# Retention units whose next scores are made before the last group-norm scaling

## The chip, the cores and the metric

One Trainium2 chip, one of its cores, float32 throughout. The metric is device time in microseconds (us) of one execution. TensorE is PE in the rows (PEld its weight loads), VectorE DVE, ScalarE ACT, GpSimd POOL; SP and ACT issue the DMAs. All engines run their own instruction streams in order and wait for one another by semaphores.

## The reference

A trunk of two layers with a gated MLP after each. The change lies in the second mixer, multi-scale retention: 4 heads, 1024 positions, query and key dimension 256, value dimension 512, a group norm over each head's 512 values, a gate and an output projection.

```python
def retention_mixer(xn, wq, wk, wv, wg, gn_gain, wo):
    q, k, v = ...                        # 4 heads; q and k rotated, k scaled
    o = chunkwise_retention(rotary(q, pos), rotary(k, pos), v)   # decayed causal scores @ v
    mu = jnp.mean(o, axis=-1, keepdims=True)
    var = jnp.mean(jnp.square(o - mu), axis=-1, keepdims=True)
    o = (o - mu) * lax.rsqrt(var + EPS) * gn_gain.astype(jnp.float32)
    o = o.reshape(Bn, S, RET_HEADS * RET_VDIM).astype(xn.dtype)
    return (jax.nn.silu(xn @ wg) * o) @ wo
```

## The kernel before

Each float32 operand of a product is held as a high and a low half (`split`: ScalarE converts the high half, at line 109; GpSimd or VectorE subtracts it to get the low half, at line 110), and each product is three passes: high x high, high x low, low x high, in this order (`PASSES`; the first name is the half of the stationary operand).

When projections q, k, v and gate are done, retention runs as eight units: for each head h, half 0 (positions 0 to 511) and half 1. One unit, in the order of the program text:

1. `scores` (L1186): four groups of 6 matmuls, 512, 384, 256 and 128 columns wide, each into a PSUM bank of the ring `b` (four banks). VectorE multiplies each by a mask into a tile `s` (L1191; three buffers), and `split` turns it into `sT`.
2. In half 0 only, `key_rows` (L1201: eight transposes into `b` banks, ScalarE and VectorE split them into `ky`) and `first_state` (L1212: 24 matmuls; L1218 and L1219 split the result into `st`), which half 1 uses.
3. `outputs` (L1236): four outputs t = 0 to 3, each in a `b` bank. Output t takes 3(t+1) matmuls, in half 1 six more with `st`. VectorE takes the group-norm statistics (L1240, L1241), GpSimd the inverse root (L152, L153), and VectorE scales the bank into `y` (L1227), one output late: the scaling of t = 3 is the returned function `finish`.
4. `gated`: four groups of four transposes of `y` (L1260) into `b` banks; VectorE multiplies each by gain and gate (L1261); `split` makes `yT`, four blocks c = 0 to 3: the high halves on ScalarE, the low halves of c = 0 and 2 on GpSimd, of 1 and 3 on VectorE.
5. `wo_sweep`: the output projection of this unit as eight steps of 12 matmuls (L328), four steps for blocks 0 and 1 (g = 0), four for blocks 2 and 3. `yT` is the stationary operand; VectorE adds each result into the residual (L333). These steps are not run there: they are the filler of the next unit. `fill(n)` runs n of them, and the tables say where: `SFILL[half]` after scores, after key_rows and after outputs, `OFILL[half]` after each output. `run(steps)` runs those left, just ahead of `gated`.

```python
SFILL = ((1, 1, 2), (1, 0, 2))
OFILL = ((0, 1, 1, 0), (1, 1, 1, 0))
```

The weights of a unit's sweep are eight blocks (`w_rows`, through `load` into `raw`, five buffers, and `hilo` into `hl`, seven buffers). With seven buffers for eight blocks per unit, the fourth block of a unit takes the buffer that the previous unit's fifth leaves, that is, after that unit's last step. A build step places instructions within each engine near the text's order but not exactly in it; the rows of the order below are what stands in the built programs.

Of the kernel before, what the change touches and what calls it, by code (L numbers as in the profile page):

```python
# [41 lines left out]
SFILL = ((1, 1, 2), (1, 0, 2))  # L42
# [32 lines left out]
def trunk(tc, a):  # L75
# [28 lines left out]
    def f(ap):  # L104
        return ap.bitcast(F32)

    def split(hi, lo, src, eng=None):

        act.copy(hi, src)  # L109
        (eng or pool).tensor_tensor(lo, src, f(hi), ALU.subtract)  # L110
# [18 lines left out]
    def hilo(src, into=None, eng=None):  # L129
        hl = wp.tile([P, 2, 512], "hl", HL, F32R) if into is None else into  # L130
        split(hl[:, 0, :], hl[:, 1, :], src, eng)
        return hl
# [5 lines left out]
    def row_block(w, r, c0):  # L138

        return load(w[r * P : (r + 1) * P, c0 : c0 + 512])  # L140
# [5 lines left out]
    def w_rows(w, r):  # L146
        return [hilo(row_block(w, r, hf * 512)) for hf in range(2)]
# [173 lines left out]
    def sweep(lhs, ws, tiles, bank, after=None):  # L321
        n = len(ws)
        for t in tiles:
            for hf in range(2):
                o = bank()
                for j in range(n):
                    for i, (ls, w) in enumerate(PASSES):
                        pe.matmul(  # L328
                            o, lhs[j](ls, t), ws[j][hf][:, w, :],
                            start=(j == 0 and i == 0), stop=(j == n - 1 and i == 2),  # L330
                        )
                xs = xb[:, t, hf * 512 : (hf + 1) * 512]
                dve.tensor_tensor(xs, xs, o, ALU.add)  # L333
            if after:
                after(t)
            yield

    def run(gen):
        for _ in gen:
            pass  # L340
# [294 lines left out]
    def filler():  # L635
        for c in range(4):
            while at["heads"] <= c:
                yield
            yield from gated_conv(c)
        while at["values"] < 4 or at["pairs"] < 3:  # L640
            yield
        vp.close()
        xtp.close()
        mix["mp"] = Pool("mp")
        mix["ab"] = Pool("ab")
        gather((1, 3, 5, 7, 0, 2, 4), mix["ab"])
        for js in ((1, 3), (5, 7)):
            for _ in project(js, (1, 3, 5, 7, 0, 2, 4, 6), u_bank):
                yield from (None,) * 4

    steps = filler()

    def fill(n):
        for _ in range(n):
            next(steps, None)
# [36 lines left out]
    def b_bank():  # L692
        return ps.tile([P, 512], "b", 4)
# [467 lines left out]
    wo = a["ret_wo"][0]  # L1161

    def fetch_q(h, half):
        q = rt[0].tile([P, 2, 2, HALF], "q", 2, dt=F32R)
        sync.dma_start(out=f(q), in_=qscr[4 * h + 2 * half])
        return q

    def fetch_k(h, half):

        k, kf = rt[1].tile([P, 2, 2, HALF], "k", dt=F32R), None  # L1170
        sync.dma_start(out=f(k), in_=qscr[4 * h + 2 * half + 1])
        if half == 0:
            kf = rt[1].tile([P, 2, HALF], "kf")
            sync.dma_start(out=kf, in_=kscr[h])
        return k, kf
# [3 lines left out]
    def scores(q, k):  # L1179
        sT = rt[3].tile([P, 2, 1280], "sT", dt=F32R)  # L1180
        for j in range(4):
            n = HALF - j * P
            b = b_bank()
            for d in range(2):
                for i, (ks, qs) in enumerate(PASSES):
                    pe.matmul(  # L1186
                        b[:, :n], k[:, ks, d, j * P : (j + 1) * P], q[:, qs, d, j * P :],
                        start=(d == 0 and i == 0), stop=(d == 1 and i == 2),
                    )
            t = wk.tile([P, HALF], "s", 3)  # L1190
            dve.tensor_tensor(t[:, :n], b[:, :n], unit0["tri"][:, :n], ALU.mult)  # L1191
            split(sT[:, 0, SOFF[j] : SOFF[j] + n], sT[:, 1, SOFF[j] : SOFF[j] + n], t[:, :n], (pool, dve)[j % 2])
        return sT

    def key_rows(kf):

        kn = rt[3].tile([P, 4, HALF], "ky", dt=F32R).rearrange("p t (s d) -> p t s d", s=2)
        for t in range(4):
            pt = b_bank()
            for d in range(2):  # L1200
                pe.transpose(pt[:, d * P : (d + 1) * P], kf[:, d, t * P : (t + 1) * P], ident)  # L1201
            act.copy(kn[:, t, 0, :], pt[:, :256])
            dve.tensor_tensor(kn[:, t, 1, :], pt[:, :256], f(kn[:, t, 0, :]), ALU.subtract)
        return kn

    def first_state(kn, v):

        pd = [o_bank(), o_bank()]
        for t in range(4):
            for d in range(2):  # L1210
                for i, (ks, vs) in enumerate(PASSES):
                    pe.matmul(  # L1212
                        pd[d], kn[:, t, ks, d * P : (d + 1) * P], v[:, vs, t, :],
                        start=(t == 0 and i == 0), stop=(t == 3 and i == 2),
                    )
        st = rt[3].tile([P, 2, 2, HALF], "st", dt=F32R)
        for d in range(2):
            act.copy(st[:, 0, d, :], pd[d])  # L1218
            dve.tensor_tensor(st[:, 1, d, :], pd[d], f(st[:, 0, d, :]), ALU.subtract)  # L1219
        return st  # L1220
# [28 lines left out]
    def gated(h, y, gt, last):  # L1249
        if last:  # L1250
            t = h_tile()
            yT = [t[:, :, i * HALF : (i + 1) * HALF] for i in range(2)]
            yT += [u_tile().bitcast(F32R).rearrange("p (s t) -> p s t", s=2) for _ in range(2)]
        else:
            t = [yp.tile([P, 2, 2, HALF], f"y{i}", dt=F32R) for i in range(2)]
            yT = [t[c // 2][:, :, c % 2] for c in range(4)]
        for c in range(4):
            pt = b_bank()
            for t in range(4):
                pe.transpose(pt[:, t * P : (t + 1) * P], y[:, t, c * P : (c + 1) * P], ident)  # L1260
            dve.scalar_tensor_tensor(gt[:, c, :], pt, gncol(h, c), gt[:, c, :], ALU.mult, ALU.mult)  # L1261
            split(yT[c][:, 0], yT[c][:, 1], gt[:, c, :], (pool, dve)[c % 2])
        return yT

    def wo_sweep(half, h, yT, g, tiles, after=None):
        def lhs(j):
            return lambda s, t: yT[2 * g + j][:, s, (t - 4 * half) * P : (t - 4 * half + 1) * P]

        return sweep(
            [lhs(j) for j in range(2)], [w_rows(wo, h * 4 + 2 * g + j) for j in range(2)], tiles, o_bank, after  # L1270
        )

    def fetch_v(h, half, queue=act):
        v = rt[4 if half else 2].tile([P, 2, 4, HALF], "v", dt=F32R)
        for s in range(2):
            queue.dma_start(out=f(v[:, s]), in_=vscr[2 * h + half, :, s])
        return v

    def fetch_g(h, half):
        t, ts = rt[3].tile([P, 4, HALF], "gt"), slice(half * HALF, (half + 1) * HALF)  # L1280
        sync.dma_start(out=t, in_=scr[4 * h : 4 * h + 4, :, ts].rearrange("a p t -> p a t"))
        return t
# [25 lines left out]
    for h in range(4):  # L1308
        for n, block in enumerate(blocks):
# [6 lines left out]
            steps = strassen(a[name][0], c0, c0 + P, xc, Both, ((o_bank if n in (1, 4) else b_bank),), us, lay=1)  # L1316
            if h == n == 0:
                steps, us = nxt["head"]
# [10 lines left out]
    q, (k, kf) = unit0["q"], unit0["k"]  # L1329
    v, gt = unit0["v"], fetch_g(0, 0)  # L1330
    steps = iter(())
    for n, (h, half) in enumerate(units):
        more = n + 1 < len(units)
        sT = scores(q, k)
        fill(SFILL[half][0])
        if half == 0:
            kn = key_rows(kf)
            fill(SFILL[half][1])
            st = first_state(kn, v)
        if more:  # L1340
            q2, (k, kf) = fetch_q(*units[n + 1]), fetch_k(*units[n + 1])
        y, finish = outputs(half, q, v, sT, st)
        if more:
            q = q2
            fill(SFILL[half][2])
            v = fetch_v(*units[n + 1])
        finish()
        if more:
            run(steps)
        else:  # L1350
            fill(2)
        yT = gated(h, y, gt, not more)
        if not more:
            run(steps)
            nrm = Norming(a["ffn_norm"][1:2])
            nrm.play("q0 r0 q1")
        if more:
            gt = fetch_g(*units[n + 1])
            tiles = range(4 * half, 4 * half + 4)
            steps = chain(*[wo_sweep(half, h, yT, g, tiles) for g in range(2)])  # L1360
    for p in (yp, rt[4], rt[3], rt[2], rt[1], rt[0]):
        p.close()
    open_xc()
# [54 lines left out]
```

## Time and profile before

| | us |
|---|---|
| median of 3 runs (2721.56 to 2728.98) | 2725.92 |
| the profiled execution | 2726.38 |
| its span, first to last instruction | 2724.6 |
| TensorE busy | 2645.2 (97% of the span) |
| VectorE, ScalarE, GpSimd busy | 1915.8, 1189.9, 795.9 |
| mean granted TensorE clock | 0.993 |

The page gives, engine by engine, the busy time and its share of the span. The timeline lists an engine's instructions in order of time, runs of like ones merged, with the idle time ahead of them and what ended it. Retention's units run from 1708.9 us to about 2027 us. A granted clock of 1.00 is 2.4 GHz, 0.50 is 1.2 GHz.

### The profile page before, as it was taken

The page shows a single profiled execution, that of the slowest core. Times are in us where ns is not written, and L with a number is a line of the kernel's source. Part 1 is how long each engine was busy: PE and PEld are TensorE (multiplying, and loading weights), DVE is VectorE, ACT ScalarE, POOL GpSimd, SP SyncE. Part 2 cuts the span into 40 slices and gives each one's busy share as a digit, 9 for nine tenths or more (in the row PEclk, how much of TensorE's full clock was granted, in tenths as well). Part 3 has the DMA queues.
Part 4 walks back from the last instruction along what each step waited for, and adds up shares of the span by engine and source line. Part 5 has one row for each costly group of instructions (what it writes and reads, how often), then busy time and mean ns, then how long its engine had stood idle before and what let it go on. Part 6 is the DMA issues. An engine that isn't in the chain of part 4 may idle for free. (4 is left out here: it accounts for less than half of the span.)

```text
span 2724.6 us, 34990 instructions
## 1 busy us (share of the span) xinstructions
PE 2645.2 (97%) x12793; PEld 2166.0 (80%) x12793; DVE 1915.8 (70%) x2950; ACT 1189.9 (44%) x2050; POOL 795.9 (29%) x603
## 2 busy tenths in 40 slices
PE   8999999899999999989999999899999999999999
PEld 6877777778888888868888888788877888887887
DVE  4247776687777789697575765466678777777986
ACT  4345543454444444364444434222235444445444
POOL 6721113533333400032222122344454333331000
PEclk9999999999999999999999999899999999999999
DMA  5310012122222274424554546655422222225654
GB/s 171 104 48 28 24 35 79 38 75 89 74 89 74 86 266 154 152 84 160 176 178 151 195 150 219 244 210 186 155 73 60 78 85 72 88 74 187 206 174 154
DMA packets 258785, 336.74 MB, mean 124 GB/s; under 512 B 15121, under 2 KB 182197, under 8 KB 252469
## 3 DMA queue, kind: packets, MB, share of 16 engines
q1 hardware_dynamic: 224428, 246.94, 28.4%
q10 hardware_dynamic: 34184, 87.57, 8.8%
q8 instruction: 100, 1.64, 0.2%
q14 instruction: 73, 0.59, 0.1%
HBM read 257.38 MB, written 77.07 MB: 123 GB/s over the span
## 5 line engine op out<-in xcount | busy, mean ns | idle before, releaser
L110 POOL TENSOR_TENSOR hl<-raw,hl 128x512 fp32r<-128x512 f32 x347 | 580.9, 1688 | 1250.9 <-ACT hl L109 1231.0
L245 PE MATMUL b<-xc,hl 128*128 128x512 f32 (+1 forms) x2652 | 606.2, 388 | 10.7 <-ACT u L305 5.7
L245 PE MATMUL o<-xc,hl 128*128 128x512 f32 (+1 forms) x2568 | 590.7, 389 | 12.9 <-DVE hl L110 3.3
L245 PEld LDWEIGHTS b<-xc,hl 128*128 128x128 f32 x2652 | 485.9, 189 | 125.2 <-ACT u L305 7.0
L245 PEld LDWEIGHTS o<-xc,hl 128*128 128x128 f32 x2568 | 473.4, 190 | 123.6 <-DVE hl L110 4.2
L109 ACT CAST hl<-raw 128x512 fp32r<-128x512 f32 (+1 forms) x440 | 264.9, 609 | 508.7 <-PE o L328 151.7
L110 DVE TENSOR_TENSOR hl<-s,hl 128x512 fp32r<-128x512 f32 x309 | 223.6, 727 | 222.0 <-ACT hl L109 222.0
L972 DVE SCALAR_TENSOR_TENSOR u<-u,cc,u 128x1022 f32<-128x1022 f32 (+1 forms) x176 | 263.4, 1521 | 0.9
L109 ACT CAST hl<-s 128x512 fp32r<-128x512 f32 x309 | 189.7, 619 | 136.8 <-PE b L245 47.2
L458 PE MATMUL u<-xT,hl 128*128 128x512 f32 x576 | 166.1, 410 | 0.0
L328 PE MATMUL o<-hl,y 128*128 128x512 f32 x672 | 163.6, 397 | 0.0
L905 PE MATMUL o<-hl,hl 128*128 128x512 f32 x600 | 146.3, 394 | 5.0 <-DVE hl L110 3.5
L328 PEld LDWEIGHTS o<-hl,y 128*128 128x128 f32 x672 | 125.6, 188 | 29.4 <-POOL y L110 0.2
L905 PEld LDWEIGHTS o<-hl,hl 128*128 128x128 f32 x600 | 111.3, 188 | 34.4 <-DVE hl L110 7.1
L333 DVE TENSOR_TENSOR xb<-xb,o 128x512 f32<-128x512 f32 x160 | 105.0, 680 | 38.0 <-PE o L328 37.9
L458 PEld LDWEIGHTS u<-xT,hl 128*128 128x128 f32 x576 | 99.4, 189 | 20.7 <-issue 5.7
L970 ACT ACTIVATE u<-u,cc 128x1024 f32<-128x1024 f32 x88 | 100.9, 1151 | 31.3 <-DVE u L312 31.3
L109 ACT CAST hl<-h 128x512 fp32r<-128x512 f32 (+1 forms) x124 | 70.0, 581 | 95.0 <-PE o L905 28.2
L1063 PE MATMUL o<-hl,xc 128*128 128x256 f32 x768 | 95.4, 282 | 0.9 <-DVE hl L110 0.8
L1063 PEld LDWEIGHTS o<-hl,xc 128*128 128x128 f32 x768 | 93.8, 188 | 1.8 <-DVE hl L110 1.0
L110 DVE TENSOR_TENSOR hl<-h,hl 128x512 fp32r<-128x512 f32 (+1 forms) x124 | 78.4, 647 | 21.9 <-ACT hl L109 21.7
L152 POOL TENSOR_SCALAR rr<-ss 128x1 f32<-128x1 f32 (+1 forms) x48 | 13.8, 287 | 254.8 <-ACT s L163 235.9
(220 smaller groups left out, 4009.4 us busy)
## 6 DMA issues: line engine op xcount, KB each, us to landing
raw<-in_ffn_w_up SPq DMA_DIRECT2D x176, 256.0 KB, 3.1
raw<-in_ffn_w_down SPq DMA_DIRECT2D x176, 256.0 KB, 3.3
hs<-u ACTq DMA_DIRECT2D x44, 512.0 KB, 2.7
h<-hs SPq DMA_DIRECT2D x44, 512.0 KB, 6.4
raw<-in_even_w_in SPq DMA_DIRECT2D x73, 256.0 KB, 2.8
qscr<-h ACTq DMA_DIRECT2D x16, 1024.0 KB, 4.0
vscr<-u ACTq DMA_DIRECT2D x32, 512.0 KB, 3.8
raw<-in_ret_wo SPq DMA_DIRECT2D x64, 256.0 KB, 3.2
```

The lines of the kernel that those rows point to most:

```text
L109: act.copy(hi, src)
L110: (eng or pool).tensor_tensor(lo, src, f(hi), ALU.subtract)
L152: pool.tensor_scalar(out, ss, 1.0 / n, EPS, ALU.mult, ALU.add)
L245: pe.matmul(u, hl[:, ws, k * P : (k + 1) * P], xc[b][:, xs, k, cols_], start=(first and k == 0 and i == 0), stop=(k == 3 and i == 2), skip ...
L328: pe.matmul(o, lhs[j](ls, t), ws[j][hf][:, w, :], start=(j == 0 and i == 0), stop=(j == n - 1 and i == 2),)
L333: dve.tensor_tensor(xs, xs, o, ALU.add)
L458: pe.matmul(u, hl(ws, k), xT[:, xs, k, hf * 512 : (hf + 1) * 512], start=(k == 0 and i == 0), stop=(k == KT - 1 and i == 2),)
L905: pe.matmul(o, l[:, ls, c * P : (c + 1) * P], r[:, ws, :], start=(start and i == 0), stop=(stop and i == 2), skip_group_check=True,)
L970: act.mul(c, u, wcol(2, jj))
L972: dve.scalar_tensor_tensor(c[:, d:], u[:, :-d], wcol(2 - d, jj), c[:, d:], ALU.mult, ALU.add)
L1063: pe.matmul(u[t // 2][:, c : c + 256], xc[b][:, xs, k, ts], hl[name][k // 2][:, ws, k % 2 * 256 : k % 2 * 256 + 256], start=(first and k = ...
```

## The change

The scores of unit n+1 are made in unit n, behind its four outputs and the two filler steps that follow, and ahead of `finish`. The step that stood behind the scores (`SFILL[half][0]`, one in both halves) now stands behind `finish`. The first scores, and the load and split of the first sweep's four weight blocks, stand ahead of the loop. All else, the tables too, is as it was.

```diff
-    def wo_sweep(half, h, yT, g, tiles, after=None):
+    def wo_sweep(half, h, yT, g, tiles, after=None, ws=None):
         ...
-        return sweep(
-            [lhs(j) for j in range(2)], [w_rows(wo, h * 4 + 2 * g + j) for j in range(2)], tiles, o_bank, after
-        )
+        ws = ws or [w_rows(wo, h * 4 + 2 * g + j) for j in range(2)]
+        return sweep([lhs(j) for j in range(2)], ws, tiles, o_bank, after)
...
     steps = iter(())
+    sT = scores(q, k)
+    ws = [w_rows(wo, j) for j in range(2)]
     for n, (h, half) in enumerate(units):
         more = n + 1 < len(units)
-        sT = scores(q, k)
-        fill(SFILL[half][0])
         if half == 0:
             kn = key_rows(kf)
             fill(SFILL[half][1])
...
             fill(SFILL[half][2])
             v = fetch_v(*units[n + 1])
+            sT = scores(q, k)
         finish()
+        fill(SFILL[half][0])
         if more:
             run(steps)
...
-            steps = chain(*[wo_sweep(half, h, yT, g, tiles) for g in range(2)])
+            steps = chain(*[wo_sweep(half, h, yT, g, tiles, ws=None if n or g else ws) for g in range(2)])
```

TensorE from the last output of unit 0 into unit 1, where no filler step exists yet, before and then after (`b_` names are banks; L1236 outputs, L1260 transposes of `y`, L1186 scores, L328 the sweep):

```order
L1236 MATMUL b_15275<-v_15047,sT_15129 128x512 x12
L1260 MATMUL b_15302<-ident_67,ky_15230 128x128 x3
L1260 MATMUL b_15310<-ident_67,ky_15230 128x128 x3
L1260 MATMUL b_15318<-ident_67,ky_15230 128x128 x3
L1260 MATMUL b_15302<-ident_67,ky_15230 128x128
L1260 MATMUL b_15310<-ident_67,ky_15230 128x128
L1260 MATMUL b_15318<-ident_67,ky_15230 128x128
L1260 MATMUL b_15326<-ident_67,ky_15230 128x128 x4
L1186 MATMUL b_15377<-q_15226,k_15228 128x512 x6
```

```order
L1236 MATMUL b_15295<-v_15047,sT_15129 128x512 x12
L1186 MATMUL b_15320<-q_15246,k_15248 128x512 x6
L1186 MATMUL b_15331<-q_15246,k_15248 128x384 x6
L1186 MATMUL b_15342<-q_15246,k_15248 128x256 x6
L1186 MATMUL b_15353<-q_15246,k_15248 128x128 x6
L1260 MATMUL b_15367<-ident_67,ky_15250 128x128 x4
L1260 MATMUL b_15375<-ident_67,ky_15250 128x128 x4
L1260 MATMUL b_15383<-ident_67,ky_15250 128x128 x4
L1260 MATMUL b_15391<-ident_67,ky_15250 128x128 x4
L1236 MATMUL b_15428<-v_15316,sT_15319 128x512 x3
L1236 MATMUL b_15428<-st_15241,q_15246 128x512 x6
```

The scores moved from behind the transposes of `y` to ahead of them; behind the transposes stand the nine matmuls of unit 1's first output, and the sweep's first step follows them.

TensorE from unit 1's transposes into unit 2 (a first half, so key_rows follow), before and then after:

```order
L1260 MATMUL b_15675<-ident_67,ky_15443 128x128 x4
L1186 MATMUL b_15726<-q_15437,k_15439 128x512 x6
L1186 MATMUL b_15737<-q_15437,k_15439 128x384 x6
L1186 MATMUL b_15748<-q_15437,k_15439 128x256 x6
L1186 MATMUL b_15759<-q_15437,k_15439 128x128 x6
L328 MATMUL o_15770<-hl_15687,y_2777_15649 128x512 x3
L328 MATMUL o_15770<-hl_15697,y_2777_15649 128x512 x3
```

```order
L1260 MATMUL b_15720<-ident_67,ky_15427 128x128 x4
L1201 MATMUL b_15771<-ident_67,kf_15425 128x128 x2
L328 MATMUL o_15791<-hl_15732,y_2786_15694 128x512
L1201 MATMUL b_15776<-ident_67,kf_15425 128x128 x2
L328 MATMUL o_15791<-hl_15732,y_2786_15694 128x512 x2
L1201 MATMUL b_15781<-ident_67,kf_15425 128x128 x2
L328 MATMUL o_15791<-hl_15742,y_2786_15694 128x512 x2
L1201 MATMUL b_15786<-ident_67,kf_15425 128x128 x2
L328 MATMUL o_15799<-hl_15737,y_2786_15694 128x512 x2
```

Between the transposes and the sweep's first step stood 24 matmuls of the scores; now the eight transposes of key_rows stand there, mixed with the step's own matmuls.

GpSimd at the same place, before and then after (`hl` the weights' low halves, `y` the low halves of blocks 0 and 2, `sT` those of the scores):

```order
L110 TENSOR_TENSOR hl_15702<-raw_15700,hl_15702 128x512
L110 TENSOR_TENSOR hl_15707<-raw_15705,hl_15707 128x512
L110 TENSOR_TENSOR hl_15712<-raw_15710,hl_15712 128x512
L110 TENSOR_TENSOR hl_15717<-raw_15715,hl_15717 128x512
L110 TENSOR_TENSOR y_2777_15649<-gt_15334,y_2777_15649 128x512
L110 TENSOR_TENSOR y_2778_15650<-gt_15334,y_2778_15650 128x512
L110 TENSOR_TENSOR sT_15725<-s_15733,sT_15725 128x512
L110 TENSOR_TENSOR sT_15725<-s_15755,sT_15725 128x256
```

```order
L110 TENSOR_TENSOR hl_15747<-raw_15745,hl_15747 128x512
L110 TENSOR_TENSOR hl_15752<-raw_15750,hl_15752 128x512
L110 TENSOR_TENSOR hl_15757<-raw_15755,hl_15757 128x512
L110 TENSOR_TENSOR hl_15762<-raw_15760,hl_15762 128x512
L110 TENSOR_TENSOR y_2786_15694<-gt_15399,y_2786_15694 128x512
L110 TENSOR_TENSOR y_2787_15695<-gt_15399,y_2787_15695 128x512
```

The four weight halves stand ahead of the two `y` halves in both; the `sT` halves moved from behind them to some places ahead (not shown).

ScalarE ahead of unit 0's state, before and then after:

```order
L1202 CAST ky_15174<-b_15190 128x256
L109 CAST hl_15363<-raw_15361 128x512
L109 CAST hl_15368<-raw_15366 128x512
L1218 CAST st_15221<-o_15195 128x512
L1218 CAST st_15221<-o_15196 128x512
```

```order
L1202 CAST ky_15194<-b_15210 128x256
L109 CAST hl_15408<-raw_15406 128x512
L109 CAST hl_15413<-raw_15411 128x512
L1218 CAST st_15241<-o_15215 128x512
L1218 CAST st_15241<-o_15216 128x512
```

Only the names differ: the sixth and seventh weight blocks are converted ahead of the state in both, and SP's queue issues its loads up to there in the same order too.

## Rows read from the trace of the kernel before

**Rows 1.** The page, part 1: busy time, share of span, instructions.

```profile
PE 2645.2 (97%) x12793; PEld 2166.0 (80%) x12793; DVE 1915.8 (70%) x2950; ACT 1189.9 (44%) x2050; POOL 795.9 (29%) x603
```

**Rows 2.** Windows: stretch, length; busy us per engine (instructions); clock, DMA share, GB/s.

```profile
1727.30:1744.90 17.60, 10.04 (x40) 8.47 (x41) 11.24 (x22) 3.59 (x6) 7.04 (x12) 0.61 0.52 192
1744.90:1779.90 35.00, 35.00 (x152) 28.26 (x152) 18.46 (x33) 4.92 (x10) 10.46 (x14) 1.00 0.49 180
1780.00:2020.00 240.00, 239.99 (x1143) 198.88 (x1142) 149.28 (x255) 61.18 (x114) 109.55 (x122) 1.00 0.46 159
```

**Rows 3.** Timeline of PE, unit 0 into 1: start, us, instructions [idle before, releaser].

```profile
1720.31 6.96 PE L1236 MATMUL b<-v,sT 128*128 128x512 f32 x30
1730.55 0.47 PE L1260 MATMUL b<-ident,ky 128*128 128x128 f32 x1 [3.29 <-DVE ky L1227]
...
1738.97 6.13 PE L1186 MATMUL b<-q,k 128*128 128x512 f32 x24
1744.94 3.01 PE L328 MATMUL o<-hl,y 128*128 128x512 f32 x12
1747.79 0.86 PE L1236 MATMUL b<-v,sT 128*128 128x512 f32 x3
...
1749.87 2.96 PE L328 MATMUL o<-hl,y 128*128 128x512 f32 x12
```

**Rows 4.** Timeline of VectorE in the same stretch.

```profile
1726.63 1.29 DVE L1219 TENSOR_TENSOR st<-o,st 128x512 fp32r<-128x512 f32 x2 [10.31 <-ACT st L1218]
...
1736.70 0.81 DVE L1227 TENSOR_SCALAR ky<-b,mv,rr 128x512 f32<-128x512 f32 x1 [0.95 <-POOL rr L153]
```

**Rows 5.** Timeline of ScalarE, just ahead of unit 0's state.

```profile
1725.49 0.62 ACT L109 CAST hl<-raw 128x512 fp32r<-128x512 f32 x1 [7.67 <-DMA raw<-in_ret_wo]
```

**Rows 6.** Windows, the stretch of low clock.

```profile
1730.00:1743.60 13.60, 8.74 (x29) 7.17 (x30) 8.00 (x14) 3.10 (x5) 5.02 (x9) 0.50 0.46 167
```

**Rows 7.** Timeline of PE, unit 1 into 2, and transposes into 3.

```profile
1779.93 1.91 PE L1260 MATMUL b<-ident,ky 128*128 128x128 f32 x16
1781.59 4.04 PE L1186 MATMUL b<-q,k 128*128 128x512 f32 x24
1785.47 3.02 PE L328 MATMUL o<-hl,y 128*128 128x512 f32 x12
1788.33 1.03 PE L1201 MATMUL b<-ident,kf 128*128 128x128 f32 x8
...
1821.16 1.91 PE L1260 MATMUL b<-ident,ky 128*128 128x128 f32 x16
```

**Rows 8.** GpSimd at both places (timelines), and its groups from 1744.9 to 2019.8.

```profile
1778.72 5.04 POOL L110 TENSOR_TENSOR hl<-raw,hl 128x512 fp32r<-128x512 f32 x4 [8.01 <-ACT hl L109]
1783.69 1.78 POOL L110 TENSOR_TENSOR y<-gt,y 128x512 fp32r<-128x512 f32 x1
...
1819.99 5.05 POOL L110 TENSOR_TENSOR hl<-raw,hl 128x512 fp32r<-128x512 f32 x4 [7.65 <-ACT hl L109]
1825.00 1.75 POOL L110 TENSOR_TENSOR y<-gt,y 128x512 fp32r<-128x512 f32 x1
...
L110 POOL TENSOR_TENSOR y<-gt,y 128x512 fp32r<-128x512 f32 x12 | 20.9, 1762 | 0.0
```

**Rows 9.** ScalarE and VectorE behind unit 1's transposes (timelines).

```profile
1781.51 2.60 ACT L109 CAST y<-gt 128x512 fp32r<-128x512 f32 x4 [0.72 <-DVE gt L1261]
1780.73 2.72 DVE L1261 SCALAR_TENSOR_TENSOR gt<-b,cols,gt 128x512 f32<-128x512 f32 x4
```

**Rows 10.** PE behind two other pauses (timeline), and the clock that followed (windows).

```profile
2069.32 1.44 PE L245 MATMUL o<-xc,hl 128*128 128x256 f32 x10 [2.08 <-DVE hl L110]
1646.00 3.07 PE L245 MATMUL b<-xc,hl 128*128 128x512 f32 x12 [2.65 <-ACT u L305]
2071.30:2074.70 3.40, 2.90 (x15) 2.50 (x14) 2.52 (x5) 1.42 (x3) 2.13 (x3) 0.50 0.27 77
1646.00:1652.00 6.00, 6.00 (x38) 5.46 (x39) 6.00 (x9) 2.25 (x4) 1.88 (x2) 1.00 0.33 111
```

## The prediction

> **What bounds the kernel now.** First the page: TensorE is busy for 97% of the span [rows 1], so a change can win only where TensorE stands idle or runs at a low clock, and it loses wherever it makes TensorE wait. Next the windows over retention's units [rows 2]: from 1780 to 2020 us TensorE is busy for 239.99 of 240.00 us at clock 1.00. There is nothing to win in six of the seven passages from unit to unit. The exception is the passage from unit 0 to unit 1, 1727.3 to 1744.9 us: 10.04 us busy in 17.60, mean clock 0.61. Then the timelines around that hole. The outputs of unit 0 start at 1720.31 and last 6.96 us, to 1727.27; the first transpose waits 3.29 us for a group-norm scaling, and others wait after it [rows 3]. There is no filler yet, so the chain statistics, inverse root, scaling runs bare; it starts late because VectorE stood idle for 10.31 us until the state's halves came from ScalarE [rows 4], and ScalarE had waited 7.67 us for a weight block [rows 5]. The last scaling ends at 36.70 + 0.81 = 1737.51. Behind the first pause the clock is 0.50 for 13.60 us [rows 6], and the scores take 6.13 us there [rows 3] where they take 4.04 elsewhere [rows 7].
>
> Last, the other passages, which are full: unit 1 to 2 [rows 7]. The transposes of y start at 1779.93, the scores at 1781.59, the sweep's first step at 1785.47. So 1.66 us of transposes and 3.88 us of scores stand ahead of that step. Its first two matmuls (of the three passes) take the high half of y, its third the low half of block 0. GpSimd makes that half behind four weight halves of 1.26 us each, and is done at 1783.69 + 1.78 = 1785.47 [rows 8], which is 5.54 us after the transposes began. One matmul of a step takes (1788.33 - 1785.47) / 12 = 0.24 us, so the half is needed at 1785.95: it is 0.5 us early. That is the number on which my forecast rests: the scores are what hides GpSimd.
>
> **The change part by part.**
>
> *Same work.* The matmuls, conversions, subtractions and loads are the same in number; nothing is added or removed. SP's loads and ScalarE's conversions up to unit 0's state stand in the same order, so the "earlier" weight load costs and brings nothing: the 7.67 us wait [rows 5] stays, and so does the time of the last scaling.
>
> *Into units 2, 4 and 6 (behind a second half).* The 3.88 us of scores leave the gap between transposes and step; the eight transposes of key_rows come in, mixed into the step. What decides is when the low half of block 0 is there. GpSimd's queue still holds the four weight halves ahead of it. They wait for conversions that wait for the last use of the previous weights, in the last step ahead of the transposes, which has not moved against the transposes. So I keep 5.54 us behind the transposes' start. TensorE's side: 1.66 us of transposes, then two pairs of key_rows transposes at 1.66/16 = 0.10 each (0.42 together) and two matmuls (0.48). The first matmul needs block 0's high half, converted from 1781.51 on at 2.60/4 = 0.65 each [rows 9], so at +2.23, where TensorE would be at +1.87: 0.36 us of waiting. The third matmul is reached at 1.66 + 0.42 + 0.48 + 0.36 = +2.92 and waits until +5.54: 2.62 us. Together 3.0 us, three times: +9.0. Queued behind that waiting matmul are the last key_rows transposes and the 24 matmuls of the state; nobody further waits for them longer than TensorE does. In before this part is full, so none of it is given back.
>
> *Into units 3, 5 and 7 (behind a first half).* Here the first output of the next unit stands between transposes and step: nine matmuls, 1747.79 to 1749.87 = 2.08 us [rows 3]. The third matmul of the step is reached at 1.66 + 2.08 + 0.48 = +4.22; the low half comes at 1825.00 + 1.75 - 1821.16 = +5.59 [rows 7, 8]. That is 1.4 us, three times: +4.2. VectorE also makes that output's statistics ahead of block 3's low half, which is not needed until the second four steps. The bounds of these two terms: GpSimd takes 1.76 us for a low half of y in the mean of 12 [rows 8], while VectorE subtracts beside it, and 1.26 us for a weight half; at 1.26 each wait is 0.5 us shorter, 10.2 us for the six instead of 13.2. I take 13.2, since VectorE still subtracts there.
>
> *Into unit 1.* Four banks rotate, and the four score groups take the banks of the four outputs, so they wait for the same scalings as the transposes do now: the 3.29 us pause stays, and the last group can start only at 1737.51. But three of the groups then run between the scalings, in time that is lost now. After the last scaling: the first mask multiplication (0.68, a 512-wide pass of VectorE as in [rows 9]), its conversion (0.65) and its low half on GpSimd (1.26) free one of three buffers at 1740.1; the fourth multiplication, a quarter as wide, frees the last transposes' bank at about 1740.5. Those take 0.42, the first gate multiplication beside them 0.68, to 1741.2; the first output 2.08, the sweep's first step 2.86, to 1746.1. Before, both are done at 1749.87 [rows 3]: a gain of 3.7 us. If the first output still runs at half clock, its 2.08 us double and 1.6 are left; with the step at half clock too, it is a loss of 1.3. The most would be the whole hole: 1727.27 to 1744.94 is 17.67 us for 5.54 us of work, 12.1. I take 3.0, nearest to the worked-out chain.
>
> *The clock.* New pauses can lower it. Three pauses at full clock are shown: 3.29 us, followed by 0.50 [rows 3, 6]; 2.08 us, followed by 0.50 for 3.40 us (1.2 GHz) [rows 10]; 2.65 us, followed by 1.00 (2.4 GHz) [rows 10]. Two of three fell. Such a stretch of 3.4 us does half the work, 1.7 us lost. For the three long pauses I take two falls, +3.4 (bounds 0 and 5.1); for the three of 1.4 us, shorter than any of these, none (upper bound 5.1).
>
> The Trainium skill speaks against this term: "TensorE: Matmul & The Clock Gate", section "HAM oscillation — how this bites in real kernels", warns only of pauses of TensorE that are longer than any of those worked out here. By it none of the new pauses would cost clock, and the sum would be 10.2. This trace disagrees at 2.08 us and agrees at 2.65, so it is a rival and not the forecast.
>
> **Sum.** +9.0 + 4.2 + 3.4 - 3.0 = +13.6 us. The profiled execution took 2726.4 us (span 2724.6 and 1.8 around it, unchanged), 0.5 above the median of the three runs: 2740.0 us.
>
> **The rivals.**
>
> (B) The waits come, the clock does not fall: 13.2 - 3.0 = +10.2, 2736.6 us. For it: the 2.65 us pause without a fall. Against: the two others. 0.20.
>
> (C) The hoisted weights land earlier, as the change's words suggest, and the hole closes. Then the state's halves come up to 5.8 us sooner (ScalarE is through at 1726.1, the state's matmuls at 1720.3 [rows 3, 5]), and the gain there is 3.7 + 5.8 = 9.5: 13.2 - 9.5 = +3.7, 2730 us. Against: both queues are in the same order up to that point, so this would be a chance of the loads. 0.10.
>
> (D) Not slower: GpSimd has block 0's low half ready when TensorE asks for it. It decides from +2.9 us behind the transposes in units 2, 4 and 6, that is, if the two last weight halves (2.5 us) were done sooner or came behind. Then no wait is new and only unit 1's gain is left: -3.7, 2722.7 us; with the 1.4 us passages alone relieved, +6. For it: VectorE has the scores behind it by then, so GpSimd may run undisturbed, but that is worth 0.5 us only. Against: the order on GpSimd, and the buffer that the fourth weight block needs. 0.12.
>
> (E) All six pauses lower the clock and unit 1's gain is lost to half clock: 13.2 + 10.2 = +23.4, 2749.8 us. 0.08.
>
> **How the numbers follow.** The forecast (A) has 0.50: 2740.0. A measurement of this kernel can tell 0.3%, 8.2 us, from no change, so slower begins at about 2734.6. A and E are slower, and most of B (0.15 of 0.20): 0.73. C, the rest of B and most of D are within 0.3%: 0.22. Faster, a hole that closes without the waits, is left with 0.05. The range leaves out D (0.12) and half of E, and takes in C and the bounds of the clock: 2728 to 2750.
>
> **What would show it.** Right: in the passages into units 2, 4 and 6 TensorE idle for 2 to 3 us in front of L328, ended by POOL's L110 on y; in those into 3, 5 and 7 for about 1.4; before, these stretches are full [rows 2]. Right for unit 1: the scores ahead of the transposes, still a pause of about 3.3 us behind the outputs, and the sweep's second step reached some 3 us sooner. The clock row behind those pauses says which of A and B it is. Wrong: windows from 1780 to 2020 that stay full, or y halves of GpSimd within 3 us of the transposes; or a last scaling of unit 0 well ahead of 1737.5, which would be C.

## The result, and the profile after

The changed kernel takes 2738.57 us (median of 6 runs, 2736.82 to 2741.35) where the kernel before takes 2725.98 (6 runs beside it): a ratio of 1.005 (95% interval 1.004 to 1.0061), 12.6 us slower. The forecast was 13.6 more, 2740.0.

The page of after, its span and part 1 (answers [rows 1]):

```profile
span 2739.6 us, 34988 instructions
PE 2651.1 (97%) x12793; PEld 2169.3 (79%) x12793; DVE 1920.5 (70%) x2950; ACT 1190.0 (43%) x2050; POOL 798.0 (29%) x603
```

The same instructions, and the share of TensorE reads 97% in both pages: this view can't show what happened. The windows of after do (columns as in [rows 2]), first the way from unit 0 to 1, then the six passages behind it, units 1 to 7:

```profile
1726.00:1742.60 16.60, 11.67 (x50) 10.21 (x51) 12.57 (x24) 4.03 (x8) 7.13 (x13) 0.79 0.63 229
1780.00:2031.00 251.00, 240.08 (x1110) 196.16 (x1109) 150.22 (x248) 59.30 (x109) 108.34 (x119) 0.99 0.42 143
```

The first has a better clock than before, 0.79 against 0.61 [rows 2], and more busy time in fewer us. The second was full before; now 10.9 of its 251 us are idle. The table of waits (engine, line, what for; us, times, longest) names the releaser, first for TensorE, then for its weight loads:

```profile
PE o L328 <- POOL y L110: 10.5, 6, 2.4
PE b L1186 <- DVE ky L1227: 4.9, 3, 3.2
```

```profile
PEld o L328 <- POOL y L110: 12.8, 6, 2.7
```

Six waits of the output sweep for GpSimd's half of `y`. In the kernel before, TensorE has none of them, and its weight loads have a single short one in the same six places (waits of before):

```profile
PEld o L328 <- POOL y L110: 0.2, 1, 0.2
```

TensorE from unit 1 into 2 and from 2 into 3 (timeline; answers [rows 7]):

```profile
1779.17 1.91 PE L1260 MATMUL b<-ident,ky 128*128 128x128 f32 x16
1780.91 0.38 PE L1201 MATMUL b<-ident,kf 128*128 128x128 f32 x2
1781.42 0.50 PE L328 MATMUL o<-hl,y 128*128 128x512 f32 x1
1781.76 0.38 PE L1201 MATMUL b<-ident,kf 128*128 128x128 f32 x2
1781.90 0.48 PE L328 MATMUL o<-hl,y 128*128 128x512 f32 x1
1784.72 0.79 PE L328 MATMUL o<-hl,y 128*128 128x512 f32 x1 [2.34 <-POOL y L110]
...
1824.68 1.91 PE L1260 MATMUL b<-ident,ky 128*128 128x128 f32 x16
...
1828.52 0.63 PE L328 MATMUL o<-hl,y 128*128 128x512 f32 x2
1830.28 2.60 PE L328 MATMUL o<-hl,y 128*128 128x512 f32 x10 [1.14 <-POOL y L110]
```

In both it is the third matmul that waits, as it is the first to read the low half. Its releaser on GpSimd in the first of the two (timeline; answers [rows 8]):

```profile
1777.95 5.02 POOL L110 TENSOR_TENSOR hl<-raw,hl 128x512 fp32r<-128x512 f32 x4 [5.63 <-ACT hl L109]
1782.92 3.45 POOL L110 TENSOR_TENSOR y<-gt,y 128x512 fp32r<-128x512 f32 x2
```

Four weight halves stand ahead of the two `y` halves as before; the first of these is done at 1782.92 + 3.45 / 2 = 1784.65, 5.48 us behind the start of the transposes.

The clock behind the first two long pauses, behind the third, and behind the first short one (windows, same columns):

```profile
1784.30:1787.50 3.20, 2.78 (x9) 2.20 (x10) 1.68 (x3) 0.62 (x2) 2.07 (x2) 0.50 0.22 79
1872.90:1876.20 3.30, 3.30 (x11) 2.50 (x10) 1.67 (x4) 0.75 (x2) 0.96 (x1) 0.50 0.31 55
1959.90:1965.00 5.10, 5.04 (x24) 4.11 (x25) 3.02 (x6) 0.75 (x2) 1.71 (x2) 1.00 0.44 145
1830.30:1835.00 4.70, 4.70 (x20) 3.85 (x21) 2.66 (x5) 0.00 (x0) 2.38 (x3) 1.00 0.39 132
```

Between unit 0 and 1 (timeline of TensorE, answers [rows 3]; then one row each of VectorE and ScalarE, answering [rows 4, 5]):

```profile
1719.04 6.96 PE L1236 MATMUL b<-v,sT 128*128 128x512 f32 x30
1729.16 4.26 PE L1186 MATMUL b<-q,k 128*128 128x512 f32 x12 [3.16 <-DVE ky L1227]
1733.59 0.97 PE L1186 MATMUL b<-q,k 128*128 128x256 f32 x6 [0.16 <-DVE ky L1227]
1736.17 1.38 PE L1186 MATMUL b<-q,k 128*128 128x128 f32 x6 [1.60 <-DVE ky L1227]
1737.34 3.12 PE L1260 MATMUL b<-ident,ky 128*128 128x128 f32 x16
...
1742.62 3.06 PE L328 MATMUL o<-hl,y 128*128 128x512 f32 x12
1745.52 1.32 PE L1236 MATMUL b<-v,sT 128*128 128x512 f32 x5
```

```profile
1735.30 0.81 DVE L1227 TENSOR_SCALAR ky<-b,mv,rr 128x512 f32<-128x512 f32 x1 [0.95 <-POOL rr L153]
```

```profile
1724.10 0.62 ACT L109 CAST hl<-raw 128x512 fp32r<-128x512 f32 x1 [6.54 <-DMA raw<-in_ret_wo]
```

The pause behind the outputs stays (3.16 us), and so does the wait for the weight block. The scores now run between the scalings, and first output and first step are through 26.5 us after the outputs began (1745.52 - 1719.04), where they took 1749.87 - 1720.31 = 29.6 [rows 3]; that is 3.1 less, and with the 0.24 of one matmul that now stands ahead of this point instead of behind it, the gain is 3.3 us.

The balance, from unit 0's outputs to the start of unit 7's transposes: before 2019.79 - 1720.31 = 299.5 us, after 2031.13 - 1719.04 = 312.1. That is +12.6, as much as the medians differ by. The two profiled executions differ by more, 2739.6 - 2724.6 = 15.0 us, since the profiled one of after was the slowest of its six: 1.3 less ahead of the stretch and 3.7 more behind it. The part behind it, whose text the change leaves alone, takes 704.8 us in before, 708.5 in after and 704.1 to 707.9 in the other eight traces, so I take these 3.7 for spread between executions. I call it the retention stretch below; it holds the same matmuls in every kernel, so each experiment can be read by it.

### The profile page after: what moved, and what is told of

The parts are those of the page before. It is cut to its first block, busy times and chain, and to the rows that moved or that the text cites. A ratio compares the mean times of both kernels' runs of the same rounds, so it can differ in the third digit from the quotient of the medians.

```text
span 2739.6 us, 34988 instructions
## 1 busy us (share of the span) xinstructions
PE 2651.1 (97%) x12793; PEld 2169.3 (79%) x12793; DVE 1920.5 (70%) x2950; ACT 1190.0 (43%) x2050; POOL 798.0 (29%) x603
## 5 line engine op out<-in xcount | busy, mean ns | idle before, releaser
L328 PE MATMUL o<-hl,y 128*128 128x512 f32 x672 | 169.8, 404 | 10.9 <-POOL y L110 10.5
L328 PEld LDWEIGHTS o<-hl,y 128*128 128x128 f32 x672 | 126.8, 191 | 42.8 <-POOL y L110 12.8
```

The lines of the kernel that those rows point to most:

```text
L328: pe.matmul(o, lhs[j](ls, t), ws[j][hf][:, w, :], start=(j == 0 and i == 0), stop=(j == n - 1 and i == 2),)
```

## The experiments

The theory: in six passages the scores were what hid GpSimd's `y` half, which its queue delivers late because of the weight halves ahead of it; unit 1's gain is small because the scalings' chain remains. The main rival: hoisting the scores costs by itself (the masks on VectorE in another place, the banks). The table has the medians, the ratio to the kernel before on the same chip (its medians: 2725.98 beside after, 2725.58 beside e1 to e4, 2724.93 beside e5 to e7, 2726.41 beside e8), and the retention stretch of the profiled execution.

| run | us | ratio (95%) | stretch, us |
|---|---|---|---|
| before | | | 299.5 |
| after | 2738.57 | 1.005 (1.004 to 1.0061) | 312.1 |
| e1_unit0_only | 2723.45 | 0.9994 (0.9985 to 1.0002) | 295.6 |
| e2_swap_halves | 2730.37 | 1.0016 (1.0007 to 1.0025) | 302.6 |
| e3_keep_step | 2723.12 | 0.999 (0.9981 to 0.9999) | 295.8 |
| e4_step_first | 2749.51 | 1.0087 (1.0074 to 1.0101) | 325.3 |
| e5_state_dve | 2736.08 | 1.0038 (1.0024 to 1.0051) | 308.4 |
| e6_keep_state | 2718.99 | 0.9974 (0.9965 to 0.9984) | 291.9 |
| e7_before_state | 2723.52 | 0.9993 (0.9984 to 1.0002) | 296.1 |
| e8_weights_dve | 2727.37 | 1.0007 (0.9998 to 1.0016) | 301.0 |

**The hoist without the waits, the waits without the hoist.** The first kernel (e1) hoists the scores of unit 1 only. From unit 2 on the order is as before.

```diff
     for n, (h, half) in enumerate(units):
         more = n + 1 < len(units)
+        if n > 1:
+            sT = scores(q, k)
+            fill(SFILL[half][0])
...
-            sT = scores(q, k)
+            if n == 0:
+                sT = scores(q, k)
         finish()
-        fill(SFILL[half][0])
+        if n < 2:
+            fill(SFILL[half][0])
```

> Only unit 1's scores are made ahead of unit 0's last scaling; from unit 2 on scores and filler step stand as before. Theory (the scores are what hides GpSimd's low half of y; the hoist itself pays only where no filler exists): the six waits of L328 on GpSimd's y are gone, TensorE is full from 1780 to 2020 us, and the gain into unit 1 (3.3 us by the changed kernel's trace) is left: 2726.0 - 3.3 = 2722.7 us, ratio 0.9988. Rival (something else in the moved code costs the time, for example the first weights' load or the buffers of q, k and sT): 2730 us or more. Rival (the gain into unit 1 is nothing but luck of the clock): 2726.

Its window over units 1 to 7 is full again:

```profile
1745.00:2022.00 277.00, 277.00 (x1311) 229.43 (x1310) 171.59 (x289) 71.88 (x131) 124.36 (x137) 1.00 0.44 157
```

So the whole loss comes from the hoists into units 2 to 7. The gain that is left, 2.1 us in the medians and 3.9 in the stretch, is of the size worked out, but its interval holds no change: by time alone it isn't shown.

The second (e4) takes the kernel before and puts only the filler step ahead of the scores, so that the scores no longer hide GpSimd; nothing is hoisted.

```diff
-        sT = scores(q, k)
         fill(SFILL[half][0])
+        sT = scores(q, k)
```

> The kernel before, with the filler step ahead of the scores instead of behind them; nothing is hoisted. In the built order two to four score matmuls and then the step's first three matmuls follow the transposes. Theory: without the cover the step's third matmul waits from about 2.6 to 5.5 us behind the transposes' start in all six passages from unit 1 on, 17 us, and pauses of nearly 3 us lower the clock in about two of three (1.7 us each): 2743 to 2752 us (ratio 1.006 to 1.010). Rival (the loss belongs to the hoisted scores and their buffers): unchanged, 2726.

Waits of TensorE; one of them in the timeline; the clock behind three of them (windows):

```profile
PE o L328 <- POOL y L110: 15.6, 6, 2.6
```

```profile
1783.67 4.15 PE L328 MATMUL o<-hl,y 128*128 128x512 f32 x10 [2.57 <-POOL y L110]
```

```profile
1784.30:1787.50 3.20, 3.20 (x9) 2.52 (x8) 0.43 (x1) 0.00 (x0) 1.02 (x1) 0.50 0.31 62
1873.10:1879.70 6.60, 6.01 (x14) 4.75 (x15) 2.46 (x3) 0.00 (x0) 2.25 (x2) 0.50 0.59 202
1920.80:1924.10 3.30, 2.86 (x7) 2.28 (x8) 0.94 (x1) 0.00 (x0) 2.10 (x2) 0.50 0.27 82
```

15.6 us of waits and 12.1 busy us at half clock, worth 6.0, are 21.6 of the 23.9 us by which the medians differ (25.8 in the stretch). The loss appears without any hoist once the cover is gone, so the hoist is not needed for it; that the hoist costs nothing beside is what the kept step below shows.

**GpSimd's queue.** Two kernels change after so that the half comes sooner. In one (e2) GpSimd and VectorE exchange the four blocks, so VectorE makes block 0's low half.

```diff
-            split(yT[c][:, 0], yT[c][:, 1], gt[:, c, :], (pool, dve)[c % 2])
+            split(yT[c][:, 0], yT[c][:, 1], gt[:, c, :], (dve, pool)[c % 2])
```

> The changed kernel, with the low halves of y's blocks 0 and 2 on VectorE and those of 1 and 3 on GpSimd. Theory: TensorE asks for block 0 first, and VectorE, which has no weight halves in its queue, is done with it about 3.8 us behind the transposes' start, not 5.5; block 1 is asked for 0.7 us later. Waits of 2.4 us shrink to about 1 and those of 1.15 to about 0.6, and with pauses so short the clock falls less often: 2730 to 2733 us (ratio 1.0015 to 1.0026). Rival (GpSimd's queue is not what decides, VectorE's own backlog is): no change, 2738.

The waits of the weight loads and the window over units 1 to 7:

```profile
PEld o L328 <- DVE y L110: 3.6, 6, 0.8
PEld o L328 <- POOL y L110: 2.5, 6, 0.6
PEld o L328 <- ACT y L109: 1.1, 3, 0.4
```

```profile
1745.00:2031.00 286.00, 284.06 (x1325) 231.21 (x1324) 180.74 (x294) 72.60 (x131) 126.12 (x139) 1.00 0.44 153
```

The long waits are gone, twice as many short ones have come, for block 0 on VectorE and for block 1, now behind the weight halves; the clock of the window is 1.00. Against its own kernel before it is 4.8 us slower, not 12.6, so some 7.8 us come back.

In the other (e8) the weights' low halves go to VectorE and the `y` halves stay where they are.

```diff
+    def wo_rows(r):
+        return [[hilo(row_block(wo, r + j, hf * 512), None, dve) for hf in range(2)] for j in range(2)]
...
-        ws = ws or [w_rows(wo, h * 4 + 2 * g + j) for j in range(2)]
+        ws = ws or wo_rows(h * 4 + 2 * g)
...
-    ws = [w_rows(wo, j) for j in range(2)]
+    ws = wo_rows(0)
```

> The changed kernel, with the low halves of the output projection's weights made by VectorE instead of GpSimd; the scores stay hoisted and no step is kept back. It leaves the cover as thin as it is and takes only the queue ahead of y's low halves away; VectorE gets eight passes of 0.7 us per unit, two of them ahead of the gate multiplications. Theory (the queue on GpSimd is half of the cause, the thin cover the other): GpSimd's first low half of y is done about 3.5 to 4 us behind the transposes' start; the waits of 2.4 us shrink to 1 or less, those of 1.15 vanish, the clock falls no more behind them: 2726 to 2730 us (ratio 1.000 to 1.002). Rival (VectorE's added passes delay the gate multiplications by as much as GpSimd gains): 2735 or more.

GpSimd and TensorE in unit 1 into 2 (timelines):

```profile
1779.90 1.30 POOL L110 TENSOR_TENSOR y<-gt,y 128x512 fp32r<-128x512 f32 x1 [9.15 <-ACT y L109]
```

```profile
1777.23 1.91 PE L1260 MATMUL b<-ident,ky 128*128 128x128 f32 x16
...
1781.25 0.50 PE L328 MATMUL o<-hl,y 128*128 128x512 f32 x1 [0.43 <-POOL y L110]
```

With its queue empty GpSimd starts the half as soon as ScalarE's conversion allows, and is done 3.97 us behind the transposes' start instead of 5.48. The long wait falls from 2.34 to 0.43 us, and none is left in units 3, 5 and 7. So it is the weight halves ahead in the queue that make the half late; of the 1.51 us, 0.43 is the half itself, which takes 1.30 us here and 1.73 in after. The kernel is still not faster than before: its stretch is 5.4 us longer than that of the first experiment, of which 2.1 are pauses that the trace names (three of 0.43 and three of 0.26 or so for ScalarE's half). The other 3.3, beside VectorE's added work, I have not traced.

**Cover given back (e3).** After, but the unit's last filler step is kept behind the transposes (`fill(1)` in place of `run(steps)`, which follows `gated`).

```diff
         if more:
-            run(steps)
+            fill(1)
         else:
             fill(2)
         yT = gated(h, y, gt, not more)
+        run(steps)
         if not more:
-            run(steps)
             nrm = Norming(a["ffn_norm"][1:2])
```

> The changed kernel, with one of the two last filler steps kept back until the transposes of y are issued, so 12 matmuls (2.86 us) stand behind them as cover; since that step still uses the old weights, GpSimd gets y's first low half ahead of the new weight halves. Theory: no wait of L328 on GpSimd's y, no fall of the clock in units 1 to 7, only the gain into unit 1: about 2722.7 us, ratio 0.9988. Rival (the loss is in the hoist itself, not in the missing cover): 2735 or more. Rival (the late release of the weight buffers makes a new wait on the fourth weight block, some 1 us in six passages): 2728 to 2730.

TensorE and GpSimd, unit 1 into 2 (timelines), and the window over units 1 to 7:

```profile
1776.98 1.91 PE L1260 MATMUL b<-ident,ky 128*128 128x128 f32 x16
1778.64 3.05 PE L328 MATMUL o<-hl,y 128*128 128x512 f32 x12
1781.53 1.04 PE L1201 MATMUL b<-ident,kf 128*128 128x128 f32 x8
1782.32 3.05 PE L328 MATMUL o<-hl,y 128*128 128x512 f32 x12
```

```profile
1779.39 1.31 POOL L110 TENSOR_TENSOR y<-gt,y 128x512 fp32r<-128x512 f32 x1 [6.45 <-ACT y L109]
1780.67 4.71 POOL L110 TENSOR_TENSOR hl<-raw,hl 128x512 fp32r<-128x512 f32 x3
```

```profile
1745.00:2025.00 280.00, 280.00 (x1324) 231.75 (x1323) 175.48 (x293) 70.61 (x131) 127.86 (x139) 1.00 0.44 156
```

One old step of 2.9 us between the transposes and the new step does what 3.9 us of scores did, and more: it is also the step whose weights' buffers the next conversions wait for, and the weight halves now stand behind block 0's half (three directly), which is done 1779.39 + 1.31 - 1776.98 = 3.72 us behind the transposes' start. No wait is left, and the kernel is 2.5 us faster than before, just clear of noise.

**The hole behind unit 0.** ScalarE converts the state late because it waits for a weight block ([rows 5], and the row of after above). In e5 VectorE makes the state's high halves.

```diff
-            act.copy(st[:, 0, d, :], pd[d])
+            dve.tensor_copy(st[:, 0, d, :], pd[d])
```

> The changed kernel, with the high halves of the state made by VectorE instead of ScalarE, so that they no longer stand behind two weight conversions that wait for their loads (6.5 us of waiting in the changed kernel's trace). Theory: unit 0's statistics start some 3 to 5 us sooner, the last scaling of unit 0 ends 3 to 6 us sooner, and TensorE's passage into unit 1 shortens by as much, less what the last output's own end allows; the six later waits stay: 2732.5 to 2736 us (ratio 1.0025 to 1.004). Rival (the pause into unit 1 hangs on GpSimd's and VectorE's chain for four outputs alone, or on loads that the units need anyway): 2738.

VectorE's first scaling and what it waits for, then GpSimd and ScalarE in the same stretch (timelines):

```profile
1731.48 0.81 DVE L1227 TENSOR_SCALAR ky<-b,mv,rr 128x512 f32<-128x512 f32 x1 [4.62 <-POOL rr L153]
```

```profile
1729.25 1.29 POOL L110 TENSOR_TENSOR hl<-raw,hl 128x512 fp32r<-128x512 f32 x1 [6.82 <-ACT hl L109]
```

```profile
1728.55 0.62 ACT L109 CAST hl<-raw 128x512 fp32r<-128x512 f32 x1 [7.49 <-DMA raw<-in_ret_wo]
```

The median is 2.5 us below after's, and 1.4 if each is taken against its own kernel before; the intervals of the two ratios overlap, so by time alone this gain isn't shown. The traces show it: the way from unit 0's outputs to unit 1's transposes, which holds the same matmuls in both, falls from 60.13 to 56.24 us. The last scaling ends only 2.4 us sooner against the outputs' start (14.7 us behind it, not 17.1), below the 3 to 6 expected. VectorE no longer waits for ScalarE, but the inverse root stands on GpSimd behind the low half of the same late weight block: the wait has moved one engine on. The pause behind the outputs is 2.02 us instead of 3.16; the six later waits stay.

The kept step and this edit together, that is, the last two diffs (e6), and its window over units 1 to 7:

> Both: one filler step kept behind the transposes, and the state's high halves on VectorE. Theory: the gains are in different places and add up: 2723.1 less 3 to 6 us, 2717 to 2720 us (ratio 0.997 to 0.998). Rival (VectorE's two more passes per state make a new wait in units 2, 4 and 6, or the state's gain does not show): 2723.

```profile
1745.00:2021.00 276.00, 276.00 (x1307) 228.44 (x1306) 175.63 (x294) 67.83 (x127) 127.35 (x138) 1.00 0.44 155
```

2718.99 us, faster than both kernels: 5.9 less than before. And this edit alone, the last diff, on the kernel before (e7), to see whether it alone does this:

> The kernel before, with the state's high halves on VectorE and nothing else. Theory: the passage into unit 1 holds the transposes and the scores behind the last scaling; with the scaling 3 to 6 us sooner and the low clock shorter it gains as much: 2719 to 2723 us (ratio 0.9975 to 0.999). If this gains as much as the two together do, the hoist of unit 1's scores adds nothing to it, which is the rival.

2723.52, 1.4 us less than before and not clear of noise, so by time alone no gain is shown. By the stretch it gains 3.4 us, e3 (hoist and kept step) 3.7, and e6 with all of them 7.6: the two gains about add up, as expected for e6, and this edit alone gives about half of the sum, which speaks against the rival. One trace of each stands behind this.

## Why the prediction was right

A passage runs from one unit's transposes (16 of L1260) to the next's. By the timelines the transposes of units 1 to 7 start at 1779.93, 1821.16, 1861.70, 1902.90, 1943.44, 1984.88 and 2019.79 us in before, and at 1779.17, 1824.68, 1866.61, 1912.43, 1954.36, 1998.63 and 2031.13 in after. So the six passages grew by 4.28, 1.39, 4.62, 1.39, 2.83 and -2.41, the last +1.47 once the 3.88 us of scores that left it [rows 7] are added back; they came into the first stretch, from unit 0's outputs to unit 1's transposes, which is 60.13 - 59.62 - 3.88 = -3.37.

| term | predicted | measured |
|---|---|---|
| into units 2, 4, 6, without clock | 3 x 3.0 = 9.0 | 2.83 in the one without a fall, x 3 = 8.49 |
| clock behind two of these | 3.4 | (4.28 - 2.83) + (4.62 - 2.83) = 3.24 |
| into units 3, 5, 7 | 3 x 1.4 = 4.2 | 1.39 + 1.39 + 1.47 = 4.25 |
| into unit 1 | -3.0 | -3.37 |
| sum | +13.6 | +12.6 |

The passage without a fall is measured against one of before that is 0.24 us longer than its two likes there (41.44, 41.23 and 41.20 us). Against these it grew by 3.05; the first row would then be 9.2 and the second 2.8. Both readings lie near the forecast.

**What bounds it: right.** That the scores are what hides GpSimd is borne out three times: by after, by the step put first (waits for the same half without a hoist), and by the kept step (no waits with a hoist). That they hid it by little, 0.5 us at the matmul, fits the one weight load of before that waited 0.2 us for the half.

**Into units 2, 4 and 6: right.** The queue's time against the transposes was carried over from before, 5.54 us; it came at 5.48, and the waiting matmul started at 5.55. The pause shown is 2.34 to 2.38, not 2.62, since TensorE arrives later than the plain sum of durations says; the wait for block 0's high half was there as worked out (the first matmul at 1781.42 - 1779.17 = 2.25, predicted 2.23).

**Into units 3, 5 and 7: right.** The matmul starts at 5.60 against 5.59 worked out. The pause shown is 1.14 to 1.15, while the passage lost 1.4 to 1.5: the timeline's ends are modelled, so a passage's length is the better measure. The choice of 1.76 us for GpSimd's half over 1.26 was right too (1.73).

**The clock: the count was right, the reason wasn't known.** Two of three long pauses lowered it, as taken. It was a guess at a rate, from three pauses, and that the count came true is luck. The Trainium skill, "TensorE: Matmul & The Clock Gate", section "HAM oscillation — how this bites in real kernels", warns only of pauses longer than these; this trace disagrees, with 0.50 behind pauses of 2.34 and 2.38 us, so rival B (no fall) is out.

**Into unit 1: right.** The pause of 3.16 us stayed, the last scaling ended at 1736.11, 17.07 us behind the start of the outputs (17.20 in before), and 3.4 us came of the 12.1 that the whole hole would have given. The 3.0 was a choice between the 3.7 of the worked chain and its 1.6 at half clock; what came is near the chain. Rival C needed the weight block sooner: ScalarE still waited 6.54 us for it, so the early load changed nothing. Rival D needed GpSimd in time; e8 shows what that takes. Rival E needed six falls; there were two.

**Open:** whether unit 1's gain alone can be measured (e1's interval holds no change), and which pause lowers the clock.

## What to carry to other kernels

Before moving work out of a full stretch, ask what that work hides: find the operand that the next instruction needs, its place in the in-order queue that makes it, and by how much it was early; 0.5 us here. Where the cover goes, put other ready work in its place (one filler step did it), or take what isn't urgent from ahead of the urgent item in that queue. A late transfer holds up every engine that has an item of it in its queue: moving one step off the first engine shows the second.

## What was not expected of the hardware

- Equal pauses lowered the clock or not. With the step first, six pauses of 2.6 us in like passages were followed by 0.50 in three (shown above), 1.00 in three, of which one (windows, behind the fifth):

```profile
1966.30:1972.00 5.70, 5.70 (x32) 5.07 (x33) 3.38 (x6) 1.12 (x2) 2.37 (x2) 1.00 0.56 184
```

  In after 2.38 us stands on both sides. The length alone does not decide it. In e5, whose six passages are those of after, the same two of three long pauses lowered the clock (mean clock 0.50, 0.62 and 1.00 in the windows read behind them).
- GpSimd's 128x512 subtraction takes 1.31 us in e3 and 1.30 in e8 where VectorE reads PSUM beside it, and some 1.73 in after, where VectorE subtracts with both operands in SBUF. The Trainium skill, "GPSIMD Engine Reference", section "1. Specifications", says that the SBUF interfaces are shared with VectorE and contended by its instructions with two SBUF inputs; these rows agree. The price can fall on either engine. Here are the second half of `y` on GpSimd in e8 and VectorE's subtraction that started 0.08 us later (timelines):

```profile
1781.59 1.32 POOL L110 TENSOR_TENSOR y<-gt,y 128x512 fp32r<-128x512 f32 x1 [0.39 <-ACT y L109]
1781.67 1.79 DVE L110 TENSOR_TENSOR hl<-raw,hl 128x512 fp32r<-128x512 f32 x1
```

  GpSimd keeps its time, and VectorE takes 1.79 us where its others of this size take some 0.7.
